# State-space taps within a chunk: 64-row matmuls on the layout of U instead of block-diagonal ones

## The chip, the cores and the metric

The kernel runs on one core of one Trainium2 chip. The metric is the device time of one execution in microseconds (us), here the median of several runs. A change of less than about 0.5% of it can't be told from no change.

## What is computed

One layer of a decoder trunk on x of 256 x 1024: a projection `x @ w_in` is cut into q, k, v, z_attn, u, z_ssm and two gates; an attention branch (8 heads of 64) and a state-space branch are gated, projected, merged and normalised. The part that the change touches is the state-space branch, 32 groups of 16 channels with 64 complex states each:

```python
bu_re = jnp.einsum('bsgc,gpc->bsgp', ug, bbar_re)        # and bu_im
_, _, h_re, h_im = lax.associative_scan(combine, (a_re_t, a_im_t, bu_re, bu_im), axis=1)
y = (jnp.einsum('bsgp,gcp->bsgc', h_re, c_re.astype(f32))
     - jnp.einsum('bsgp,gcp->bsgc', h_im, c_im.astype(f32)))
y = y.reshape(B, S, W) + d_skip.astype(f32) * u.astype(f32)
```

## The kernel before, in words

**Steps.** The large products run in 80 steps or so. Each step takes one unit of weights (256 rows by 512 columns), which SP loads into one of five `raw` buffers (`load_next`, L117). ACT rounds it into `whi` (L144), DVE subtracts for the rest `wlo` (L145), both with three buffers, and TensorE does three products for one (L149, the helper `mm`, which records nearly every matmul). Step i splits the unit of step i + 2. The list `steps` holds these steps; `at(i, ...)` hangs pieces of the other work behind step i, and `AT` says where. TensorE keeps the program's order. The order of all other engines is made by a planner that simulates the kernel with priorities, the earlier in the program the higher, and with loads, splits and the evacuation of the last product (`pend`) above all else.

**The state-space branch.** Time is cut into 64 chunks (j) of 4 positions (l). `uT` holds u with channels on partitions; `s5_bounce` writes it to `scr_u` in HBM and reads it back as `U`, in which 64 partitions hold the four positions of a group's 16 channels (two halves r of 64 partitions, 8 pairs of groups each). `s5_xm` multiplies `BT` with `U` in 64 x 64 pieces of the array, `s5_x`, `s5_scan` (L492, with the decay `m4`, to which ACT writes at L488 and POOL at L489) and `s5_h` (L505 to L511) give the state `Hr`, `Hi` ahead of each chunk. `s5_kbm` (steps 27 and 28) computes the taps within a chunk, from one position to a later one of the same chunk, into a PSUM tile `kp`. `s5_kbd` (DVE, L424 and L428) spreads them to `Kbd`: for each of the four 128-channel tiles t and each distance a block-diagonal 128 x 128 matrix, with the skip term `dk` on its diagonal. `s5_yt(t)` multiplies them with `uT` and `s5_y(t)` adds the part from `Hr`, `Hi` through `CAb` (a zero-filled spread of `CA`, L433 and L436); GELU and a split to `yh`, `yl` follow. `s5_yt` and `s5_y` of the four tiles stand by turns behind steps 35 to 42.

**Around it.** In the same stretch of the program, steps 23 to 35, the attention runs: `a_scores`, `a_exp` (L587, L592 on ACT), `a_tr` (transposes, evacuated by ACT at L602 to `pt`) and `a_out`. The tag of a tile names its memory: tiles of one tag take turns in it, so `Kbd` waits until the scores have read `kl`, and `gl` of `a_out` has the tag `kT`.

Of the kernel before, what the change touches and what calls it, by code (L numbers as in the profile page):

```python
# [10 lines left out]
F32 = mybir.dt.float32  # L11
# [3 lines left out]
AF = mybir.ActivationFunctionType  # L15
ALU = mybir.AluOpType
AX = mybir.AxisListType

P = 128
S = 256  # L20
# [3 lines left out]
L = 4  # L24
NJ = S // L
# [7 lines left out]
AT = dict(bt=24, x=27, sc=23, kb=27, cb=29, tr=31, out=32, y=35)  # L33
# [10 lines left out]


C_ID, C_MK, C_J, C_OH = 0, P, P + 8, P + 8 + NPH
C_W = C_OH + 257


def bc(ap, axis, n):  # L50

    dims = [list(d) for d in ap.ap]
    dims.insert(axis, [0, n])
    return bass.AP(tensor=ap.tensor, offset=ap.offset, ap=dims)
# [3 lines left out]
def hybrid_layer_kernel(ctx: ExitStack, tc, xT, x, pT, w_in, w_ap, w_sp, w_out, par, bp, cp,  # L58
                        dsk, w_glu, w_pg, w_pp, lng, lnb, relb, cst, out):
    nc = tc.nc  # L60
    V, A, G, PE = nc.vector, nc.scalar, nc.gpsimd, nc.tensor
    pool = ctx.enter_context(tc.tile_pool(name="sb", bufs=1))
    ps = ctx.enter_context(tc.tile_pool(name="ps", bufs=1, space=bass.MemoryType.PSUM))
    dr = ctx.enter_context(tc.tile_pool(name="dr", bufs=1, space=bass.MemoryType.DRAM))
    cnt = [0]

    def T(shape, tag, dt=F32, bufs=1, nm=None):
        cnt[0] += 1
        return pool.tile(list(shape), dt, name=f"{nm or tag}_{cnt[0]}", tag=tag, bufs=bufs)

    def PS(tag, bufs):
        cnt[0] += 1
        return ps.tile([P, 512], F32, name=f"{tag}_{cnt[0]}", tag=tag, bufs=bufs)
# [4 lines left out]
    def aux():  # L78
        return PS("aux", 4)
# [9 lines left out]

    cs = T([P, C_W], "cst")  # L90
    ident = cs[:, C_ID:C_ID + P]
    mask = cs[:, C_MK:C_MK + 8]
# [55 lines left out]
    def mm(o, a, b, start, stop):  # L148
        return PE.matmul(o, a, b, start=start, stop=stop, skip_group_check=True)  # L149
# [34 lines left out]
    for c in range(4):  # L184
        t = T([P, 2, 512], "raw", bufs=NRAW)
# [21 lines left out]
    dk = T([P, 4], "dk")  # L207
# [23 lines left out]
    st5 = {}  # L231
# [176 lines left out]
    def s5_kbm(hf):  # L408
        if hf == 0:
            st5["kp"] = aux()  # L410
        p_ = st5["kp"]
        bd = st5["bd"]
        for t in range(2 * hf, 2 * hf + 2):
            for part in range(2):
                for gpt in range(4):
                    gp = 4 * t + gpt
                    mm(p_[32 * gpt:32 * gpt + 32, 64 * t:64 * t + 64], bd[:, part, gp, :],
                       st5[f"CA{part}"][:, gp, 0:4, :].rearrange("p n c -> p (n c)"),
                       part == 0, part == 1)

    def s5_kbd():
        p_ = st5["kp"]
        kb = st5["Kbd"] = T([P, 4, 4, P], "Kbd")
        V.tensor_tensor(out=kb.rearrange("p t u (g c) -> p (t u) g c", c=16),  # L424
                        in0=bc(p_[:, 0:256].rearrange("p (tu c) -> p tu c", c=16), 2, 8),
                        in1=bc(bc(mask, 1, 16), 3, 16), op=ALU.mult)
        for t in range(4):
            V.scalar_tensor_tensor(kb[:, t, 0, :], ident, dk[:, t:t + 1], kb[:, t, 0, :],  # L428
                                   op0=ALU.mult, op1=ALU.add)

    def s5_cabd(part):
        o = st5[f"CAb{part}"] = T([P, GP, 4, 32], f"CAb{part}")
        G.memset(o, 0.0)  # L433
        for g2 in range(2):
            rw = slice(64 * g2, 64 * g2 + 64)
            A.activation(o[rw, :, :, 16 * g2:16 * g2 + 16], st5[f"CA{part}"][rw, :, 1:5, :], AF.Copy)  # L436

    uT = T([P, 4, L, NJ], "uT")
    U = T([P, 8, 2, NJ], "U")
# [73 lines left out]
    yh = []  # L513
    yl = []

    def s5_yt(t):
        p_ = st5[f"yp{t}"] = aux()
        kb = st5["Kbd"]
        for tau in range(4):
            n = (4 - tau) * NJ  # L520
            mm(p_[:, tau * NJ:4 * NJ], kb[:, t, tau, :],
               uT[:, t, 0:4 - tau, :].rearrange("p l j -> p (l j)"), tau == 0, False)

    def s5_y(t):
        p_ = st5[f"yp{t}"]
        for l in range(L):
            for part, hk in ((0, "Hr"), (1, "Hi")):
                for gpt in range(4):
                    gp = 4 * t + gpt
                    mm(p_[32 * gpt:32 * gpt + 32, l * NJ:(l + 1) * NJ],  # L530
                       st5[f"CAb{part}"][:, gp, l, :], st5[hk][:, gp, :], False, l == 3 and part == 1)
        if t == 0:
            st5["y"] = T([P, 4, S], "U")
            yh.append(T([P, 4, S], "sn", F32R))
            yl.append(T([P, 4, S], "co", F32R))
        y = st5["y"]
        A.activation(y[:, t, :].rearrange("p (j l) -> p l j", l=L),
                     p_[:, 0:256].rearrange("p (l j) -> p l j", l=L), AF.Gelu)
        A.activation(yh[0][:, t, :], y[:, t, :], AF.Copy)
        V.tensor_sub(yl[0][:, t, :], y[:, t, :], yh[0][:, t, :].bitcast(F32))  # L540
# [65 lines left out]
    def a_out(hp):  # L606
        p_ = aux()
        for i in range(2):
            h = 2 * hp + i
            t = aT[h]  # L610
            rw = slice(64 * i, 64 * i + 64)
            mm(p_[rw, 0:256], vN[:, 0, 64 * h:64 * h + 64], t[:, 0:256], True, False)
            mm(p_[rw, 128:256], vN[:, 1, 64 * h:64 * h + 64], t[:, 256:384], False, True)
        if hp == 0:
            gh.append(T([P, 4, S], "qT", F32R))
            gl.append(T([P, 4, S], "kT", F32R))
        g = T([P, S], "gf", bufs=2)
        V.scalar_tensor_tensor(g, p_[:, 0:256], 0.5, zaT[:, hp, :], op0=ALU.mult, op1=ALU.mult)
        A.activation(gh[0][:, hp, :], g, AF.Copy)
        V.tensor_sub(gl[0][:, hp, :], g, gh[0][:, hp, :].bitcast(F32))  # L620
# [208 lines left out]
    def at(i, *f):  # L829
        order.setdefault(i, []).extend(f)  # L830
# [22 lines left out]
    for hp in range(4):  # L853
        at(AT["sc"] + hp, lambda hp=hp: a_scores(hp))
        at(AT["sc"] + 1 + hp, lambda hp=hp: a_exp(hp))
    at(AT["kb"], lambda: s5_kbm(0))
    at(AT["kb"] + 1, lambda: s5_kbm(1), s5_kbd)
    at(AT["cb"], lambda: s5_cabd(0), lambda: s5_cabd(1))
    for hp in range(4):
        at(AT["tr"] + hp, lambda hp=hp: a_tr(2 * hp), lambda hp=hp: a_tr(2 * hp + 1))  # L860
        at(AT["out"] + hp, lambda hp=hp: a_out(hp))
    for t in range(4):
        at(AT["y"] + 2 * t, lambda t=t: s5_yt(t))
        at(AT["y"] + 1 + 2 * t, lambda t=t: s5_y(t))
    at(44, load_x)

    pend = None
# [36 lines left out]
    nm = [T([P, 1], f"nm{s}") for s in range(2)]  # L904
# [36 lines left out]
    u = nmain  # L941
# [26 lines left out]
def _constants():  # L968
    c = np.zeros((P, C_W), np.float32)
    c[:, C_ID:C_ID + P] = np.eye(P, dtype=np.float32)  # L970
    c[:, C_MK:C_MK + 8] = (np.arange(P)[:, None] // 16 == np.arange(8)[None]).astype(np.float32)
    c[:, C_J:C_J + NPH] = np.concatenate([np.arange(5), L * np.arange(NJ)]).astype(np.float32)
    for d in range(257):
        b = d if d < 16 else min(31, 16 + int(math.log(d / 16) / math.log(8) * 16))
        c[b, C_OH + d] = 1.0
    return c


def _layout(i):
    a = lambda t: np.ascontiguousarray(np.asarray(t))  # L980
    x = a(i["x"])[0]
    gp = lambda t: t.reshape(GP, P).T
    ldt = np.broadcast_to(a(i["ssm_log_dt"])[0][:, None], (32, 64))
    par = np.stack([gp(a(i["ssm_a_re"])[0]), gp(a(i["ssm_a_im"])[0]), gp(ldt)], axis=1)
    gb = lambda t: t.reshape(GP, P, 16).transpose(1, 0, 2)
    bp = np.stack([gb(a(i["ssm_b_re"])[0]), gb(a(i["ssm_b_im"])[0])], axis=1)
    gc = lambda t: gb(t.transpose(0, 2, 1))
    cp = np.stack([gc(a(i["ssm_c_re"])[0]), gc(a(i["ssm_c_im"])[0])], axis=1)
    return dict(
        xT=a(x.T.reshape(KD, P, S).transpose(1, 0, 2)), x=a(x),  # L990
        pT=a(a(i["p"])[0, 0].T.reshape(2, P, S).transpose(1, 0, 2)),
        w_in=a(i["w_in"])[0], w_ap=a(i["w_attn_proj"])[0], w_sp=a(i["w_ssm_proj"])[0],
        w_out=a(i["w_out"])[0], par=a(par), bp=a(bp), cp=a(cp),
        dsk=a(a(i["ssm_d"])[0].reshape(4, P).T), w_glu=a(i["w_glu"])[0],
        w_pg=a(i["w_ple_gate"])[0], w_pp=a(i["w_ple_proj"])[0],
        lng=a(i["ln_g"]), lnb=a(i["ln_b"]), relb=a(i["rel_bias"]), cst=_constants())
# [15 lines left out]
```

## Time and profile before

| | |
|---|---|
| runs | 241.4, 241.86, 242.76 us; median 241.86 us |
| profiled execution | 242.09 us, span 240.3 us, granted TensorE clock 0.995 |
| TensorE busy | 230.3 us, 96% of the span, 2042 matmuls |
| DVE busy | 188.2 us, 78% |
| ACT busy | 140.2 us, 58% |
| POOL busy | 15.9 us, 7% |
| HBM traffic | 44 MB, 183 GB/s |

Read it by stages: the shares are means over stretches in which different engines end last. A float32 matmul is recorded as two instructions, one of the rounded kind (fp32r) as one. The span leaves out 1.8 us that lie around it in the profiled execution.

### The profile page before, as it was taken

The numbers are of one execution on the slowest core, as the hardware profiler recorded it, in microseconds if no ns is written. First come the engines' busy times: TensorE is split into PE (matmuls) and PEld (weight loads), VectorE is DVE, ScalarE is ACT, GpSimd is POOL, SyncE is SP. The second block draws the span as 40 slices with busy tenths as digits, with TensorE's granted clock in tenths as the row PEclk, the third lists the DMA queues.
The fourth block names the chain that finished last, engine by engine and source line by source line (L and its number), as shares of the span: only waits on it lengthen the run. The fifth ranks groups of instructions, "written<-read, shape, count | busy, mean of one in ns | idle before, by whom it ended". The sixth has DMA issues, their size and how long they took to land.

```text
span 240.3 us, 5066 instructions
## 1 busy us (share of the span) xinstructions
PE 230.3 (96%) x2042; PEld 212.6 (88%) x2042; DVE 188.2 (78%) x333; ACT 140.2 (58%) x222; POOL 15.9 (7%) x17
## 2 busy tenths in 40 slices
PE   8899999999999999999999999999999999999970
PEld 6899999999978899998998999999888889988760
DVE  2879999999899986878999744485674479997395
ACT  4847554845588389999734955335565353775021
POOL 4000000000000005000000000072000000000031
PEclk9999999999999999999999999999999999999998
DMA  5999998977634484323743663664555655660013
GB/s 162 331 343 357 354 238 242 353 232 215 196 93 118 147 255 119 110 92 97 232 150 136 207 213 110 197 245 162 189 174 191 199 202 170 186 190 0 3 44 131
DMA packets 26374, 44.37 MB, mean 185 GB/s; under 512 B 4200, under 2 KB 7280, under 8 KB 26352
## 3 DMA queue, kind: packets, MB, share of 16 engines
q1 hardware_dynamic: 26064, 43.75, 57.5%
q8 instruction: 16, 0.26, 0.4%
q10 hardware_dynamic: 288, 0.31, 0.4%
q14 instruction: 6, 0.05, 0.1%
HBM read 42.47 MB, written 1.59 MB: 183 GB/s over the span
## 4 chain that ended last, share of the span: by engine, by line
PE 77%; ACT 10%; DMA 5%; DVE 4%; SPq 2%; issue 1%; ACTq 0%
PE acc L149 68%; PE aux L149 8%; DMA raw<-in_w_in 5%; ACT whi L144 4%; ACT sc L587 2%; ACT sc L592 2%; ACT CAb L436 1%; DVE wlo L145 1%; SPq L191 1%; SPq L189 1%; DVE xb L930 1%; DVE xb L920 1%; DVE st L910 1%; DVE xb L908 1%; PE aux L598 0%
## 5 line engine op out<-in xcount | busy, mean ns | idle before, releaser
L144 ACT ACTIVATE whi<-raw 128x1024 fp32r<-128x1024 f32 (+2 forms) x71 | 70.7, 997 | 59.9 <-PE acc L149 52.9
L145 DVE TENSOR_TENSOR wlo<-raw,whi 128x1024 fp32r<-128x1024 f32 (+2 forms) x71 | 81.9, 1154 | 30.3 <-ACT whi L144 29.9
L149 PE MATMUL acc<-xh,whi 128*128 128x256 f32 x288 | 47.7, 287 | 0.8 <-ACT whi L144 0.8
L149 PE MATMUL acc<-xl,whi 128*128 128x256 f32 x288 | 45.8, 281 | 0.0
L149 PE MATMUL acc<-xh,wlo 128*128 128x256 f32 x288 | 45.6, 280 | 0.0
L149 PEld LDWEIGHTS acc<-xh,whi 128*128 128x128 f32 x288 | 39.3, 190 | 2.3 <-ACT whi L144 1.3
L149 PEld LDWEIGHTS acc<-xl,whi 128*128 128x128 f32 x288 | 39.3, 189 | 0.0
L149 PEld LDWEIGHTS acc<-xh,wlo 128*128 128x128 f32 x288 | 38.9, 188 | 0.3 <-DVE wlo L145 0.3
L149 PE MATMUL acc<-whi,xh 128*128 128x512 f32 x48 | 19.0, 395 | 0.0
L149 PE MATMUL acc<-wlo,xh 128*128 128x512 f32 x48 | 19.0, 395 | 0.0
L149 PE MATMUL acc<-whi,xl 128*128 128x512 f32 x48 | 19.0, 395 | 0.0
L149 PEld LDWEIGHTS acc<-wlo,xh 128*128 128x128 f32 x48 | 9.0, 188 | 2.2
L149 PEld LDWEIGHTS acc<-whi,xh 128*128 128x128 f32 x48 | 9.0, 188 | 2.1
L149 PEld LDWEIGHTS acc<-whi,xl 128*128 128x128 f32 x48 | 9.0, 188 | 2.1
L149 PE MATMUL acc<-whi,BT 128*128 128x512 f32 (+1 forms) x32 | 9.1, 366 | 0.0
L818 POOL TENSOR_SCALAR xb<-xb 128x1024 f32<-128x1024 f32 x2 | 5.5, 2774 | 42.2 <-DMA xb<-in_x 42.2
L916 ACT ACTIVATE rs<-mv,eps 128x1 f32<-128x1 f32 x2 | 0.6, 294 | 12.1 <-DVE mv L915 12.1
L587 ACT ACTIVATE sc<-sc,nmx 128x128 f32<-128x128 f32 (+1 forms) x16 | 7.0, 442 | 0.0
L149 PEld LDWEIGHTS acc<-whi,BT 128*128 128x128 f32 x32 | 5.7, 188 | 1.1
L193 DVE TENSOR_TENSOR xl<-sc,xh 128x256 fp32r<-128x256 f32 x8 | 3.4, 420 | 4.1 <-ACT xh L192 4.1
L908 DVE TENSOR_TENSOR xb<-acc,xb 128x512 f32<-128x512 f32 (+1 forms) x4 | 2.5, 619 | 5.0 <-PE acc L149 5.0
L928 POOL TENSOR_TENSOR xb<-xb,lng 128x512 f32<-128x512 f32 (+1 forms) x2 | 1.7, 839 | 69.8 <-ACT xb L927 69.8
(254 smaller groups left out, 407.8 us busy)
## 6 DMA issues: line engine op xcount, KB each, us to landing
raw<-in_w_in SPq DMA_DIRECT2D x36, 512.0 KB, 4.7
raw<-in_w_pg SPq DMA_DIRECT2D x8, 512.0 KB, 4.6
raw<-in_w_out SPq DMA_DIRECT2D x8, 512.0 KB, 4.5
raw<-in_w_ap SPq DMA_DIRECT2D x4, 512.0 KB, 5.0
raw<-in_w_glu SPq DMA_DIRECT2D x4, 512.0 KB, 3.9
raw<-in_w_sp SPq DMA_DIRECT2D x4, 512.0 KB, 4.1
raw<-in_w_in SPq DMA_DIRECT2D x7, 256.0 KB, 4.3
sc<-in_xT SPq DMA_DIRECT2D x8, 128.0 KB, 4.0
```

The costliest lines, as they stand in the source:

```text
L144: A.activation(h[:, k, c], r[:, k, c], AF.Copy)
L145: V.tensor_sub(l[:, k, c], r[:, k, c], h[:, k, c].bitcast(F32))
L149: return PE.matmul(o, a, b, start=start, stop=stop, skip_group_check=True)
L189: nc.sync.dma_start(xs[:, kk], xT[:, kk])
L191: nc.sync.dma_start(t[:, k, cc], units[c][:, k, cc])
L193: V.tensor_sub(xl[:, kk], xs[:, kk], xh[:, kk].bitcast(F32))
L436: A.activation(o[rw, :, :, 16 * g2:16 * g2 + 16], st5[f"CA{part}"][rw, :, 1:5, :], AF.Copy)
L587: A.activation(sc[:, h, qs[q]], sc[:, h, qs[q]], AF.Exp, bias=nmx[:, h, q:q + 1], accum_out=sm_[:, h, q:q + 1])
L592: A.activation(sc[:, h, qs[q]], sc[:, h, qs[q]], AF.Copy, scale=sm_[:, h, q:q + 1])
L818: G.tensor_scalar(late["xb"][:, s, :], late["xb"][:, s, :], ALPHA, None, op0=ALU.mult)
L908: V.tensor_tensor(out=xb[:, s, sl], in0=(yo2 if c0 else yo[s][n])[:, 0:c1 - c0], in1=xb[:, s, sl], op=ALU.add)
L910: V.bn_stats(out=stat[s][:, c // 256, :], in_=xb[:, s, c:c + 256])
```

## The change

The taps no longer make a block-diagonal matrix. `s5_kt` lays them out by ACT as `kt` (one row of 256 numbers for each position l, zero where the distance is negative; POOL zeroes it first), DVE adds the skip term, SP writes it to HBM (`scr_k`), and eight DMAs issued from POOL read it back as `tt`, whose 64-partition halves match those of `U`, beside a zeroed half. `s5_yt(t0)` handles tiles t0 and t0 + 2 at once: for each l, half of a pair of groups (g2), pair and r a matmul with 64 rows, 32 columns and 64 moving columns, alternately on the upper and the lower half of the array and into two PSUM tiles. The zeros in `tt` fill the 16 of the 32 columns that belong to the other group. `y` takes the memory of `uT` instead of `U`, and the tiles come in the order 0, 2, 1, 3.

```diff
--- before.py
+++ after.py
@@ -44,7 +44,8 @@
 
 
 C_ID, C_MK, C_J, C_OH = 0, P, P + 8, P + 8 + NPH
-C_W = C_OH + 257
+C_M16 = C_OH + 257
+C_W = C_M16 + 16
 
 
 def bc(ap, axis, n):
@@ -418,15 +419,30 @@
                        st5[f"CA{part}"][:, gp, 0:4, :].rearrange("p n c -> p (n c)"),
                        part == 0, part == 1)
 
-    def s5_kbd():
-        p_ = st5["kp"]
-        kb = st5["Kbd"] = T([P, 4, 4, P], "Kbd")
-        V.tensor_tensor(out=kb.rearrange("p t u (g c) -> p (t u) g c", c=16),
-                        in0=bc(p_[:, 0:256].rearrange("p (tu c) -> p tu c", c=16), 2, 8),
-                        in1=bc(bc(mask, 1, 16), 3, 16), op=ALU.mult)
+    kscr = dr.tile([512, 4, 64], F32, name="scr_k")
+
+    def s5_kt():
+
+        p_ = st5["kp"][:, 0:256].rearrange("p (t u c) -> p t u c", t=4, u=4)
+        kt = T([P, 4, 4, 16, 4], "kT", nm="kt")
+        G.memset(kt, 0.0)
+        for l in range(L):
+            A.activation(kt[:, :, l, :, l:4].rearrange("p t c u -> p t u c"), p_[:, :, 0:4 - l, :],
+                         AF.Copy)
+        m16 = bc(cs[:, C_M16:C_M16 + 16], 1, 4)
         for t in range(4):
-            V.scalar_tensor_tensor(kb[:, t, 0, :], ident, dk[:, t:t + 1], kb[:, t, 0, :],
-                                   op0=ALU.mult, op1=ALU.add)
+            d = kt[:, t, 0, :, 0]
+            d = bass.AP(tensor=d.tensor, offset=d.offset, ap=[list(d.ap[0]), [65, 4], list(d.ap[1])])
+            V.scalar_tensor_tensor(d, m16, dk[:, t:t + 1], d, op0=ALU.mult, op1=ALU.add)
+        nc.sync.dma_start(kscr.rearrange("(t q) l d -> q t (l d)", q=P),
+                          kt.rearrange("q t l c u -> q t (l c u)"))
+        tt = st5["tt"] = T([P, 16, 2, 64], "Kbd", nm="tt")
+        G.memset(tt[:, :, 1, :], 0.0)
+        v = kscr.rearrange("(r m c) l d -> r l c m d", r=2, c=16)
+        for r in range(2):
+            for l in range(L):
+                b0 = 64 * r + 16 * (L - 1 - l)
+                nc.gpsimd.dma_start(tt[b0:b0 + 16, :, 0, :], v[r, l])
 
     def s5_cabd(part):
         o = st5[f"CAb{part}"] = T([P, GP, 4, 32], f"CAb{part}")
@@ -513,13 +529,21 @@
     yh = []
     yl = []
 
-    def s5_yt(t):
-        p_ = st5[f"yp{t}"] = aux()
-        kb = st5["Kbd"]
-        for tau in range(4):
-            n = (4 - tau) * NJ
-            mm(p_[:, tau * NJ:4 * NJ], kb[:, t, tau, :],
-               uT[:, t, 0:4 - tau, :].rearrange("p l j -> p (l j)"), tau == 0, False)
+    def s5_yt(t0):
+
+        for t in (t0, t0 + 2):
+            st5[f"yp{t}"] = aux()
+        tt = st5["tt"].rearrange("p m z d -> p (m z d)")
+        for l in range(L):
+            for g2 in range(2):
+                for gpt in range(4):
+                    for r in range(2):
+                        t = t0 + 2 * r
+                        gpp = 4 * (t % 2) + gpt
+                        rw = slice(64 * r, 64 * r + 64)
+                        o = 128 * (2 * gpp + g2) - 64 * g2 + l
+                        mm(st5[f"yp{t}"][32 * gpt:32 * gpt + 32, l * NJ:(l + 1) * NJ],
+                           tt[rw, o:o + 125:4], U[rw, gpp, g2, :], l == 0 and g2 == 0, False)
 
     def s5_y(t):
         p_ = st5[f"yp{t}"]
@@ -529,8 +553,8 @@
                     gp = 4 * t + gpt
                     mm(p_[32 * gpt:32 * gpt + 32, l * NJ:(l + 1) * NJ],
                        st5[f"CAb{part}"][:, gp, l, :], st5[hk][:, gp, :], False, l == 3 and part == 1)
-        if t == 0:
-            st5["y"] = T([P, 4, S], "U")
+        if "y" not in st5:
+            st5["y"] = T([P, 4, S], "uT", nm="y")
             yh.append(T([P, 4, S], "sn", F32R))
             yl.append(T([P, 4, S], "co", F32R))
         y = st5["y"]
@@ -854,14 +878,15 @@
         at(AT["sc"] + hp, lambda hp=hp: a_scores(hp))
         at(AT["sc"] + 1 + hp, lambda hp=hp: a_exp(hp))
     at(AT["kb"], lambda: s5_kbm(0))
-    at(AT["kb"] + 1, lambda: s5_kbm(1), s5_kbd)
+    at(AT["kb"] + 1, lambda: s5_kbm(1), s5_kt)
     at(AT["cb"], lambda: s5_cabd(0), lambda: s5_cabd(1))
     for hp in range(4):
         at(AT["tr"] + hp, lambda hp=hp: a_tr(2 * hp), lambda hp=hp: a_tr(2 * hp + 1))
         at(AT["out"] + hp, lambda hp=hp: a_out(hp))
-    for t in range(4):
-        at(AT["y"] + 2 * t, lambda t=t: s5_yt(t))
-        at(AT["y"] + 1 + 2 * t, lambda t=t: s5_y(t))
+    for t in range(2):
+        at(AT["y"] + 4 * t, lambda t=t: s5_yt(t))
+        at(AT["y"] + 1 + 4 * t, lambda t=t: s5_y(t))
+        at(AT["y"] + 3 + 4 * t, lambda t=t: s5_y(t + 2))
     at(44, load_x)
 
     pend = None
@@ -970,6 +995,7 @@
     c[:, C_ID:C_ID + P] = np.eye(P, dtype=np.float32)
     c[:, C_MK:C_MK + 8] = (np.arange(P)[:, None] // 16 == np.arange(8)[None]).astype(np.float32)
     c[:, C_J:C_J + NPH] = np.concatenate([np.arange(5), L * np.arange(NJ)]).astype(np.float32)
+    c[:, C_M16:C_W] = (np.arange(P)[:, None] % 16 == np.arange(16)[None]).astype(np.float32)
     for d in range(257):
         b = d if d < 16 else min(31, 16 + int(math.log(d / 16) / math.log(8) * 16))
         c[b, C_OH + d] = 1.0
```

## Rows read from the trace of the kernel before

**Rows 1.** The page, part 1: busy us, share of span, instructions, by engine.

```profile
PE 230.3 (96%) x2042; PEld 212.6 (88%) x2042; DVE 188.2 (78%) x333; ACT 140.2 (58%) x222; POOL 15.9 (7%) x17
```

**Rows 2.** The chain that ended last: start, length in us, what.

```profile
91.78 1.39 ACT sc L592 x4
...
102.72 0.95 ACT CAb L436
...
108.00 1.07 ACT whi L144
...
112.35 0.38 ACT pt L602
...
112.77 1.24 PE aux L149 x7
...
156.78 61.37 PE acc L149 x372
```

**Rows 3.** Windows: busy us (instructions) by engine, PEclk, DMA share, GB/s.

```profile
108.00:112.00 4.00, 4.00 (x36) 4.00 (x36) 2.91 (x4) 4.00 (x7) 0.00 (x0) 1.00 0.13 18
112.00:116.00 4.00, 3.77 (x31) 3.21 (x30) 4.00 (x6) 3.32 (x7) 0.12 (x1) 1.00 0.84 253
```

**Rows 4.** Timeline of PE, stage of y: start us, us, matmul groups.

```profile
130.93 0.63 PE L149 MATMUL acc<-xh,wlo 128*128 128x256 f32 x4
131.49 1.10 PE L149 MATMUL aux<-BT,CAb 128*32 128x64 f32 x64
132.52 0.74 PE L149 MATMUL acc<-xh,whi 128*128 128x256 f32 x4
...
134.99 0.63 PE L149 MATMUL acc<-xh,wlo 128*128 128x256 f32 x4
135.46 1.31 PE L149 MATMUL aux<-uT,Kbd 128*128 128x256 f32 x8
136.57 0.70 PE L149 MATMUL acc<-xh,whi 128*128 128x256 f32 x4
```

**Rows 5.** Timeline of PE, the 64 x 64 matmuls on U.

```profile
101.67 0.69 PE L149 MATMUL aux<-U,BT 64*64 64x64 f32 x32
102.30 0.74 PE L149 MATMUL acc<-xh,whi 128*128 128x256 f32 x4
```

**Rows 6.** Timeline of PE, the tap matrices themselves.

```profile
98.07 0.65 PE L149 MATMUL aux<-C,Bbd 128*32 128x64 f32 x32
98.65 0.74 PE L149 MATMUL acc<-xh,whi 128*128 128x256 f32 x4
```

**Rows 7.** Lines of ACT by form, 60 to 160 us: busy us, mean ns.

```profile
L592 ACT ACTIVATE sc<-sc,sms 128x256 f32<-128x256 f32 x8 | 4.0, 494 | 0.0
...
L592 ACT ACTIVATE sc<-sc,sms 128x128 f32<-128x128 f32 x8 | 3.1, 387 | 0.0
...
L537 ACT ACTIVATE U<-aux 128x256 f32<-128x256 f32 x4 | 2.6, 640 | 1.4 <-PE aux L149 1.4
```

**Rows 8.** Timeline of DVE: the spreading to Kbd, the scan, the state.

```profile
100.78 2.28 DVE L424 TENSOR_TENSOR Kbd<-aux,cst 128x2048 f32<-128x2048 f32 x1
...
104.17 1.13 DVE L428 SCALAR_TENSOR_TENSOR Kbd<-cst,dk,Kbd 128x128 f32<-128x128 f32 x4
...
117.54 2.28 DVE L492 TENSOR_TENSOR_SCAN A<-B,A 128x1024 f32<-128x1024 f32 x1
...
129.73 0.68 DVE L511 TENSOR_TENSOR BT<-BT,Ct 128x512 f32<-128x512 f32 x1
```

**Rows 9.** Tile U: its DMA issues (ns min/median/max, first/last start us), landing.

```profile
L449 SPq DMA_DIRECT2D U<-scr_u x8: 302/442/590, 27.8 to 34.1; - x8
...
DMA to landing us min/median/max: 4.9/6.6/7.8
```

**Rows 10.** DMA issues: count, KB each, median us to landing.

```profile
scr_u<-uT SPq DMA_DIRECT2D x1, 512.0 KB, 5.7
```

**Rows 11.** Timeline of POOL.

```profile
115.62 0.12 POOL L489 MEMSET B<- 128x16 f32 x1 [21.60 <-DVE A L482]
```

## The prediction

> **What bounds the kernel now.** I read the busy shares first: TensorE is busy 96% of the span and no other engine over 78% [rows 1], at a granted clock of 0.995, its upper level. So what counts is first how long TensorE works on the taps, and then whether a moved instruction makes it wait. For the second the chain that ended last tells where TensorE is not alone: it runs along ACT from 91.78 (and a little before) to 112.73, through the exponentials' scaling (L592), the `CAb` copies (L436), a weight split (L144) and `pt` (L602), and only then goes over to TensorE at 112.77 [rows 2]. The windows say how tight this is: from 108 to 112 both ACT and TensorE are busy for all 4.00 us; from 112 to 116 TensorE is busy 3.77, that is, it waited 0.23 us, for `pt` [rows 3]. Before this point every microsecond given to ACT is one that TensorE waits; after it ACT has room (3.32 of 4 us). From 156.78 on the chain is TensorE for 61 us [rows 2], and nothing of the change lies there.
>
> **What the taps cost now.** One `s5_yt` is 8 instructions, from 135.46 to the next step's first matmul at 136.57: 1.11 us. They stream 2 x (256 + 192 + 128 + 64) = 1280 columns, 0.87 ns each, one after the other. The group behind it takes 0.70 instead of 0.63 [rows 4]. So about 1.18 us a tile, 4.7 us for four.
>
> **What they cost after.** 256 recorded instructions with 64 moving columns each, which by 0.87 ns would take 56 ns alone, 14 us in all. They needn't run alone. `s5_y` issues 64 of that moving length, 32 columns wide, to four column strips by turns, and takes 1.03 us, from 131.49 to 132.52 [rows 4]; the tap matrices take 0.58 us for 32 of the same shape, 98.07 to 98.65 [rows 6]. So 8 turns of four take 0.45 us, 56 ns a turn, as long as one alone: four run at once. Do the upper and the lower 64 rows run at once too? The 64 x 64 matmuls on `U` say so: two row halves by two column halves by turns, 32 in 0.63 us [rows 5]; one row half at a time would be 16 turns, 0.9 us. So I take eight at once, which no row shows as such: the 128 instructions of one `s5_yt` are 16 turns, as in `s5_y`, 1.03 us. A change of the array's division costs at both ends: the group behind `s5_y` takes 0.74 for 0.63, and `s5_y` begins 131.49 where the rhythm of a group (134.99 to 135.46, 0.47) from 130.93 on would have it at 131.40 [rows 4]; 8 turns of the 64-row form took 0.63 against 0.58 [rows 5, 6]. That is 1.03 + 0.11 + 0.09 + 0.05 = 1.28 us, twice 2.5 to 2.6. **TensorE gains 4.7 - 2.5 = 2.2 us.** If only four run at once, each call has 16 more turns of 56 ns: 4.3 us, a gain of 0.4. Strided weights (every fourth number of `tt`) appear in no row; I price them at nothing, since the turns are set by the moving columns, and the four-at-once case is their upper bound.
>
> A rule of the Trainium skill speaks against so many small matmuls: the page "TensorE: Matmul & The Clock Gate", section "Wait — 56ns, not 53.3ns?", has for one matmul a floor of about 25 ns from start to start. By it 256 would take 6.4 us, and the change would lose 1.7 us instead. The trace does not agree: 64 in 1.03 us are 16 ns [rows 4].
>
> **What ACT gets.** Four copies out of PSUM, of 256, 192, 128 and 64 columns (the rows l of `kt`), behind `s5_kbm(1)`. L592 takes 0.494 for 256 columns and 0.387 for 128 [rows 7], so by a straight line 0.44 for 192 and 0.33 for 64, 1.65 us together; back to back four of L592 (two of each size, 1.76 busy) take 1.39 in the chain [rows 2], 0.09 less apiece. So 1.65 - 0.37 = 1.3 us. The writes go to every fourth number; L537, which writes so too and also computes GELU, takes 0.640 for 256 [rows 7], 1.3 times as much: upper bound 1.7. Where do they stand? `kp` is ready at about 98.7 [rows 6], and in the program they come before `CAb`, `a_tr` and thus before `pt`, so the planner will put them before `pt` wherever exactly. There ACT has no gap. **TensorE waits 1.3 us more** (bounds 0 and 1.7; 0 if four copies of like size, such as `CAb`, are put behind `pt` in return).
>
> **What DVE gets.** It loses 2.28 us of L424 and 1.13 of L428 [rows 8] and gets four of 64 columns for the four of 128 of L428, so it gains between 2.28 and 3.41 us. In that stretch the chain is ACT's [rows 2], so it is worth nothing on the path.
>
> **What SP and POOL get.** SP: one issue to `scr_k`, 512 KB, which waits for `kt`. Behind it stand weight loads. With five buffers and a split two steps ahead of use the load of a unit may start three steps before its split, and a step is some 4 us here (130.93 to 134.99 with what lies between [rows 4]): the wait is covered up to about 12 us less a landing, and would cost TensorE whatever lies above. POOL: two memsets in a stretch where it is idle (21.60 us ahead of L489 [rows 11]), then eight loads which wait for `scr_k`, and behind them, as I expect of the planner, the memset of `m4` at L489 (115.62 now [rows 11]), on which the scan at 117.54 depends [rows 8]. Timing: `kt` is written by ACT by about 109.3 and by DVE by 110.5. The bounce of u to `scr_u` took 5.7 us to land [rows 10]: 116.2. An issue of the eight loads to `U` took SP 0.442 us [rows 9]; no row shows one on POOL, and I take the same: 3.5 us, POOL is free at 119.7. The loads land 6.6 us after issue [rows 9]: 126.3. TensorE wants them at 127.3 + 1.3 = 128.6. The scan would have been at 118.8 and is 0.9 us late; the first half of the state is ready at 130.41 (L511 [rows 8]) and wanted at 131.49, so 1.1 us late costs nothing. Both just fit. I take **0**, with -0 and +4 as bounds (below).
>
> **The sum.** -2.2 + 1.3 + 0 = -0.9 us. The profiled execution, 242.09 with 1.8 us outside its span, becomes 241.2; it lies 0.23 above the median of 241.86, which becomes **241.0**. The rest of the program, stream of weights and tail, is as before: `y` in the memory of `uT` is free long before, and the last tile comes behind the same step 42.
>
> **Rivals.**
> *ACT's copies cost nothing.* For it: the planner orders by simulated time, and the real ACT is behind it; four `CAb` copies, 0.95 us and more each [rows 2], are wanted only at 131. If some move behind `pt`, or the taps' copies do, the whole 2.2 us stay: 239.7. Against: the program's order, by which `kt` comes before `CAb` and `pt`.
> *Four at once.* If a row half waits for the other (both write the same partitions, of two PSUM banks), the gain is 0.4: 241.86 - 0.4 + 1.3 = 242.8. Against: rows 5.
> *POOL is the bound (slower).* If an issue costs POOL 1 us in place of 0.44, it is free at 124.2; the scan, and with it all that is queued behind it on DVE, starts 5.3 us late, `s5_y(0)` waits 5.3 - 1.1 = 4.2 us, and the loads, landing by 130.8, cost `s5_yt(0)` 2.2 of these already. That gives 245. It decides from 0.5 us per issue, or `scr_k` landing 0.3 us later: close. Against: the planner could put the memset first, or the wait could be half of it, 243.
>
> The Trainium skill has a rule for this rival, on the page "SBUF — State Buffer", section "SBUF: two separate sides": the descriptors of a DMA issued from GpSimd are written by GpSimd itself, and a DVE instruction in a two-port mode keeps it from its port meanwhile. By it the loads could be held off where DVE is busy all the time, as from 112 to 116 [rows 3], and the time would be that of this rival; no run here shows a load from POOL yet.
>
> **Chances.** Main case 0.40 (240.4 with half of ACT's cost hidden, 241.6 with its upper bound and a short wait), ACT free 0.22, four at once 0.10, POOL late 0.28. The line for faster is 240.65, for slower 243.07, which is the 0.5% that can be told from no change. Faster: 0.22 + 0.10 of the main case = 0.32. Slower: 0.24 of POOL late + 0.04 = 0.28. Within: 0.40. The range leaves out the far end of POOL late and a little below the best case: 239.4 to 244.5.
>
> **What would show it.** TensorE: 128 matmuls of 64 x 32 per call in about 1.03 us (1.9 if four at once). ACT: four copies before `pt`, and TensorE's wait ahead of `a_out(0)` growing from 0.23 to 1.5 us. POOL: eight issues between 116 and 120, L489 behind them, no wait of TensorE ahead of steps 35 and 36. I am wrong if the planner reorders this stage at large, or if the row halves exclude each other.

## The result and the profile after

The changed kernel takes 245.25 us (median of 4 runs, 244.16 to 245.81) against 241.76 us; the ratio is 1.0128, 95% interval 1.0093 to 1.0162 (the quotient of two medians, here 1.0144, differs a little from the ratios given here and below and lies within their intervals). It is slower, and above my range of 239.4 to 244.5. The profiled execution took 245.81 us (before: 242.09), with a span of 243.6 us and a granted clock of 0.991.

The first part of the page, to be held against [rows 1]: 224 matmuls more, yet TensorE is busy 0.9 us less and its share falls from 96% to 94%. It works less and waits more.

```profile
PE 229.4 (94%) x2266; PEld 210.2 (86%) x2266; DVE 186.5 (77%) x332; ACT 141.7 (58%) x226; POOL 23.3 (10%) x27
```

What it waits for, from 92 to 165 us, by releaser: us in total, times, longest. Before, this list had one entry, 0.2 us for `pt`, the 0.23 us of [rows 3].

```profile
PE acc L150 <- ACT whi L145: 1.2, 1, 1.2
PE aux L150 <- DVE BT L523: 0.6, 1, 0.6
PE acc L150 <- DVE wlo L146: 0.5, 1, 0.5
PE aux L150 <- DVE BT L527: 0.5, 1, 0.5
PE acc L150 <- issue: 0.5, 1, 0.5
```

So there are three places. I lay the two traces side by side from the first `U,BT` block (93.21 before, 94.03 after) to the stretch of 372 matmuls that nothing of the change touches (156.78 and 160.12): 63.6 us before, 66.1 after, 2.5 more, and 61.37 us for the stretch in both [rows 2]. Cut by blocks on TensorE, from a block's first start to the next one's:

| us | before | after | difference |
|---|---|---|---|
| transposes, step 32, `a_out(0)` | 5.06 | 6.97 | +1.91 |
| taps (four calls; two calls) | 4.58 | 3.15 | -1.43 |
| step behind `s5_yt(0)` and `s5_y(0)` | 4.04 | 5.36 | +1.32 |
| step behind `s5_yt(2)`; behind `s5_yt(1)` | 3.02 | 3.81 | +0.79 |
| all other blocks | | | -0.08 |

The first and the last of these blocks begin and end with the starts of the following lines of TensorE, before and then after (the last line is cut short by its view's window, which ends at 153):

```profile
108.88 0.27 PE L598 MATMUL aux<-cst,sc 128*128 128x128 f32 x1
113.94 0.33 PE L598 MATMUL aux<-cst,sc 128*128 128x128 f32 x1
...
144.56 0.72 PE L149 MATMUL acc<-qT,whi 128*128 128x256 f32 x4
147.58 1.10 PE L149 MATMUL aux<-BT,CAb 128*32 128x64 f32 x64
```
```profile
109.60 0.27 PE L622 MATMUL aux<-cst,sc 128*128 128x128 f32 x1
116.57 0.33 PE L622 MATMUL aux<-cst,sc 128*128 128x128 f32 x1
...
148.31 0.74 PE L150 MATMUL acc<-qT,whi 128*128 128x256 f32 x4
152.12 1.09 PE L150 MATMUL aux<-BT,CAb 128*32 128x64 f32 x63
```

The other 1.2 us of the two profiled executions are 0.8 us in the first 94 us and 0.4 us outside the span. The first `U,BT` block stands at 92.6 to 93.2 us in the four profiles of the kernel before and of runs made from it, and at 92.8 to 94.0 in the ten of the changed kernel and its variants, 94.0 being the highest. TensorE's waits for `whi` in the first 90 us are 1.8 us here and 0.8 before, but 0.8 to 1.4 us over the first four profiles and 0.5 to 2.0 over the ten: at least part of the 0.8 us is the scatter of single executions. The 0.4 us outside the span are not: all four executions of the changed kernel have 2.1 to 2.2 us there, and 31 of the kernel before, those timed with run 1, have 1.7 to 1.8. What makes them, no run shows.

**First place.** ACT (start us, us, what), before and then after:

```profile
108.00 1.06 ACT L144 ACTIVATE whi<-raw 128x1024 fp32r<-128x1024 f32 x1
108.97 1.48 ACT L592 ACTIVATE sc<-sc,sms 128x128 f32<-128x128 f32 x4
```
```profile
103.53 4.25 ACT L452 ACTIVATE CAb<-C 64x1024 f32<-64x1024 f32 x4
107.79 1.09 ACT L750 ACTIVATE Bbd<-acc 128x512 f32<-128x512 f32 x2
108.76 1.36 ACT L430 ACTIVATE kt<-aux 128x256 f32<-128x256 f32 x4
110.14 0.80 ACT L616 ACTIVATE sc<-sc,sms 128x128 f32<-128x128 f32 x2
110.85 1.04 ACT L145 ACTIVATE whi<-raw 128x1024 fp32r<-128x1024 f32 x1
```

Before, the split `whi` of this step began at 108.00, right behind `Bbd`. Now the four copies into `kt` and two of the exponentials' scalings (L616, the line 592 of before) stand ahead of it. TensorE is out of work at 110.71:

```profile
111.94 0.74 PE L150 MATMUL acc<-xh,whi 128*128 128x256 f32 x4 [1.23 <-ACT whi L145]
...
113.68 0.74 PE L150 MATMUL acc<-xh,wlo 128*128 128x256 f32 x4 [0.53 <-DVE wlo L146]
```

**Second place.** POOL's loads, `m4`, and then DVE's queue up to the two operands that `s5_y(0)` waits for:

```profile
114.60 4.64 POOL L445 DMA_DIRECT2D tt<-scr_k  x8 [18.87 <-DMA scr_k<-kt]
119.23 0.15 POOL L505 MEMSET B<- 128x16 f32 x1
```
```profile
119.31 0.42 DVE L642 SCALAR_TENSOR_TENSOR gf<-aux,zaT 128x256 f32<-128x256 f32 x1
120.93 1.23 DVE L146 TENSOR_TENSOR wlo<-raw,whi 128x1024 fp32r<-128x1024 f32 x1 [1.20 <-ACT whi L145]
122.07 0.42 DVE L642 SCALAR_TENSOR_TENSOR gf<-aux,zaT 128x256 f32<-128x256 f32 x1
122.41 0.42 DVE L644 TENSOR_TENSOR kT<-gf,qT 128x256 fp32r<-128x256 f32 x1
122.97 0.42 DVE L644 TENSOR_TENSOR kT<-gf,qT 128x256 fp32r<-128x256 f32 x1 [0.15 <-ACT qT L643]
123.32 4.46 DVE L508 TENSOR_TENSOR_SCAN A<-B,A 128x1024 f32<-128x1024 f32 x2
...
135.16 0.69 DVE L527 TENSOR_TENSOR BT<-BT,Ct 128x512 f32<-128x512 f32 x1
```

The memset is done at 119.38, but the scan begins at 123.32: DVE's order is the planner's, fixed beforehand, and in it the scan, which had begun at 117.54 [rows 8], now stands behind a split, two gates and two products. L527 (the line 511 of before) comes 5.4 us later than in [rows 8].

**Third place, and the taps.** TensorE:

```profile
129.89 1.64 PE L150 MATMUL aux<-U,tt 64*32 64x64 f32 x128
131.46 0.72 PE L150 MATMUL acc<-xh,whi 128*128 128x256 f32 x4
...
135.06 0.32 PE L150 MATMUL aux<-BT,CAb 128*32 128x64 f32 x8 [0.61 <-DVE BT L523]
135.90 0.99 PE L150 MATMUL aux<-BT,CAb 128*32 128x64 f32 x56 [0.53 <-DVE BT L527]
...
149.84 0.28 PE L150 MATMUL acc<-qT,whi 128*128 128x256 f32 x1
150.62 0.62 PE L150 MATMUL acc<-qT,whi 128*128 128x256 f32 x3 [0.51 <-issue]
```

A call takes 1.57 us (129.89 to 131.46). At 150 us TensorE stands still with nothing that it waits for. From 148 to 150 us the DMA queues show what else went on, a block of instruction code being loaded:

```profile
q8 instruction: 1, 0.02, 3.0%
```

Whether that holds TensorE up isn't shown: in the eighth run such a block came at 145.97, in its second call of the taps, and TensorE did not stand still there.

### The profile page after: what moved, and what is told of

Read it like the earlier page. It is cut to its first block, busy times and chain, and to the rows that moved or that the text cites. A ratio compares the mean times of both kernels' runs of the same rounds, so it can differ in the third digit from the quotient of the medians.

```text
span 243.6 us, 5557 instructions
## 1 busy us (share of the span) xinstructions
PE 229.4 (94%) x2266; PEld 210.2 (86%) x2266; DVE 186.5 (77%) x332; ACT 141.7 (58%) x226; POOL 23.3 (10%) x27
## 4 chain that ended last, share of the span: by engine, by line
PE 72%; ACT 9%; DVE 8%; DMA 7%; SPq 2%; issue 1%; ACTq 0%; DVEq 0%
PE acc L150 66%; PE aux L150 5%; DMA raw<-in_w_in 5%; ACT whi L145 2%; ACT sc L611 2%; DVE wlo L146 2%; DMA Ct<-in_pT 2%; ACT CAb L452 2%; ACT sc L616 2%; SPq L192 1%; SPq L190 1%; DVE xb L955 1%; DVE xb L945 1%; DVE st L935 1%; DVE xb L933 1%
## 5 line engine op out<-in xcount | busy, mean ns | idle before, releaser
L842 POOL TENSOR_SCALAR xb<-xb 128x1024 f32<-128x1024 f32 x2 | 6.5, 3276 | 37.7 <-DMA xb<-in_x 37.7
```

The source lines that it names most:

```text
L842: G.tensor_scalar(late["xb"][:, s, :], late["xb"][:, s, :], ALPHA, None, op0=ALU.mult)
```

## The experiments

Theory A: the four copies on ACT make TensorE wait for the splits, and by making `kt` late they make POOL's loads, `m4` and the scan late too; the taps themselves gain. Theory B, the first rival: the loads on POOL alone are to blame. Theory C: the matmuls are not worth what they seem, or bring costs of their own. Times beside before's on the same chip; "ACT stretch" is the first row of the table above (5.06 before, 6.97 after).

**1. The taps alone.** `s5_kt` cut down to a zeroed `tt`: no copies on ACT, no skip term, no transfers, so the taps' part of the result is left out.

```diff
-        kt = T([P, 4, 4, 16, 4], "kT", nm="kt")
...
-        G.memset(tt[:, :, 1, :], 0.0)
...
+        G.memset(tt, 0.0)
```

> The new taps without their preparation: the four copies to kt, the skip term, the write to HBM and the eight loads are left out, tt is zeroed once, so y lacks the taps within a chunk. It shows what TensorE gains by itself. Theory A (the loss is in the preparation: ACT, the order on DVE, POOL): TensorE waits no more than in the kernel before ahead of a_out(0) and ahead of s5_y(0), each call of s5_yt takes 1.57 us as in the changed kernel, so two calls take 3.1 us for 4.6 before: 240.3 us, 1.5 below the kernel before. Rival B (the small matmuls themselves cost what is lost, in what follows them): 243 to 245 us.

Measured: 241.64 us against 241.90, ratio 0.9978 (0.9958 to 0.9997). The two calls take 3.15 us and nothing waits at `s5_y(0)`, but the ACT stretch is 5.61, not 5.06, and the step behind `s5_yt(1)` has 0.4 us more. So the taps do gain 1.4 us, and something other than the copies takes 0.55 of it back. ACT shows where: all four scalings now stand ahead of `whi`, which before went first.

```profile
108.00 1.50 ACT L596 ACTIVATE sc<-sc,sms 128x128 f32<-128x128 f32 x4
109.40 2.94 ACT L145 ACTIVATE whi<-raw 128x1024 fp32r<-128x1024 f32 x3
```

**2 to 4. `m4` on DVE, the copies on DVE, both.** In the changed kernel:

```diff
-        G.memset(m4[:, :, 0:1], 0.0)
+        V.memset(m4[:, :, 0:1], 0.0)
```
```diff
-            A.activation(kt[:, :, l, :, l:4].rearrange("p t c u -> p t u c"), p_[:, :, 0:4 - l, :],
-                         AF.Copy)
+            V.tensor_copy(kt[:, :, l, :, l:4].rearrange("p t c u -> p t u c"), p_[:, :, 0:4 - l, :])
```

> The zero column of m4 is written by DVE instead of POOL, all else as in the changed kernel; so the scan no longer depends on POOL behind its eight issues, and the planner may put it earlier on DVE. Theory A (s5_y(0) waited because the scan was planned late for POOL's sake): the scan starts 2 to 3 us earlier against its step, TensorE's two waits in s5_y(0), 0.61 and 0.53 us, go, and the time is 1.1 to 1.3 us below the changed kernel, 244.0. Rival (the state is late because DVE is full, whatever POOL does): the waits stay, 245.2.

> The four copies from PSUM to kt are done by DVE instead of ACT, all else as in the changed kernel. Theory A (TensorE's waits ahead of step 32, 1.23 and 0.53 us, come from the four copies in ACT's full queue, 1.3 us, and from DVE's wait for them ahead of the weights' rest): these waits shrink to 0.5 us in all, 243.9 to 244.3. Rival (the stage is late for another reason, the order as a whole): no change, 245.2.

> Both edits: copies to kt and the zero column of m4 on DVE. If the two waits are separate and each theory holds: the sum of both gains, 2.2 to 2.6 us, 242.6 to 243.0, still not below the kernel before. If one wait takes the place of the other: 243.9 or more.

Measured: 243.88, 242.19 and 242.22 us (ratios 1.0058, 1.0001 and 1.0007, each within 0.0036). With `m4` on DVE the waits at `s5_y(0)` are gone and those in the ACT stretch stay. With the copies on DVE both are gone (0.5 us of waiting for `whi` is left, 0.9 in the fourth run), though `m4` is still POOL's and still behind the loads:

```profile
108.36 4.64 POOL L444 DMA_DIRECT2D tt<-scr_k  x8 [13.84 <-DMA scr_k<-kt]
115.13 0.13 POOL L504 MEMSET B<- 128x16 f32 x1 [2.13 <-DVE A L497]
```

The loads start 6.2 us sooner, and the memset waits for DVE, not for them. This is more than I expected of the third run (243.9 to 244.3): both losses hang on the same four copies, and the fourth run adds nothing. Theory B falls as it stands: the loads are the same, and begun sooner they no longer hurt. That they hurt when they are late, by keeping `m4` behind them, is what the second run shows.

The second run shows one thing more, and its time is near the 244.0 that I expected in part by luck. After the same two waits (1.23 and 0.53 us) its groups of four come 0.86 us apart, against 0.47, and the granted clock falls (columns as in [rows 3]; the first row is of the changed kernel, the second of this run):

```profile
112.00:116.00 4.00, 3.47 (x26) 3.10 (x28) 4.00 (x6) 3.82 (x7) 1.40 (x3) 1.00 0.64 197
```
```profile
112.00:116.00 4.00, 3.47 (x19) 3.22 (x20) 4.00 (x6) 2.98 (x5) 2.52 (x5) 0.63 0.65 207
```

Step 32 took 5.06 us there against 3.82. A wait of this size may thus cost 1.2 us on top, by TensorE being put to its lower level (1.2 GHz) for part of it, or may not. The profiled execution of the second run thus gained 1.3 us at `s5_y(0)` and 0.8 where the changed kernel stood still at 150 us, and lost 1.3 in the ACT stretch.

**5 to 7. `CAb` behind `pt`.** A small DVE instruction that reads the first `pt` writes the 1.0 by which the `CAb` copies multiply; in the changed kernel, in the same with the copies into `kt` on DVE, and in the kernel before. The copies' place in the program goes from step 29 to step 32 with it.

```diff
+            V.tensor_scalar(st5["one"], aT[0][:, 0:1], 0.0, 1.0, op0=ALU.mult, op1=ALU.add)
...
-            A.activation(o[rw, :, :, 16 * g2:16 * g2 + 16], st5[f"CA{part}"][rw, :, 1:5, :], AF.Copy)
+            A.activation(o[rw, :, :, 16 * g2:16 * g2 + 16], st5[f"CA{part}"][rw, :, 1:5, :], AF.Copy,
+                         scale=st5["one"][rw])
```

> The changed kernel with one thing moved: the four CAb copies are made to wait for the first pt (a small DVE instruction that reads pt writes the scale they multiply by), so that ACT does them behind pt and the four kt copies no longer come on top of CAb ahead of it. Theory A (ACT's extra copies stand ahead of the splits and of pt, TensorE waits there, and the same delay makes kt, the loads from POOL and thus the scan late): in the changed kernel CAb takes ACT 4.25 us ahead of kt, so all behind it is some 4 us earlier: the waits of 1.23 us on whi and 0.53 us on wlo ahead of step 32 go (that stretch 6.97 falls to 5 to 5.5 us), the waits of 1.1 us in and ahead of s5_y(0) go or fall below 0.3, and the time is 242.0 to 242.8 us. Rival C (the two losses have other causes, such as the loads from POOL holding DVE or SP's queue): waits stay, 245 us.

> As the run before, and the four copies into kt by DVE in place of ACT, so that ACT has less ahead of pt than in the kernel before. Theory A: the stretch with the transposes, step 32 and a_out(0) is at most that of the kernel before, 5.06 us, perhaps 4.6; no wait at s5_y(0); taps 1.43 us less than before; instruction loading costs 0.4 to 0.5 us. So 240.6 to 241.1 us, about 1 us under the kernel before. Rival: what is gained on ACT comes back as a wait for DVE (wlo), as it did with m4 on DVE: 242.2, as with the DVE copies alone.

> The kernel before with the CAb copies behind pt and nothing else: it tells how much of the run before is not the change's. Theory A: TensorE waited 0.2 to 0.6 us for ACT in that stretch of the kernel before, which goes; 241.2 to 241.6 us. Rival: no difference, 241.8, since DVE's wlo ends last there anyway.

Measured: 245.94, 244.94 (the median of three; a fourth took 247.17) and 245.78 us against 241.74, all slower (ratios 1.0177, 1.0128 and 1.0175, each within 0.0073); I was wrong by 3 to 5 us in each. The ACT stretch did fall, to 4.28, 4.28 and 4.39 us, and `s5_y(0)` no longer waits. But ACT does the four copies in one go, and the next `pt` waits behind them, here in the kernel before with that edit (ACT, then TensorE's waits):

```profile
113.82 4.62 ACT L439 ACTIVATE CAb<-C,one 64x1024 f32<-64x1024 f32 x4
118.46 0.87 ACT L606 ACTIVATE pt<-aux 128x384 f32<-128x384 f32 x2
```
```profile
PE aux L149 <- ACT pt L606: 2.5, 1, 2.5
```

After it the granted clock was 0.57 from 120 to 124 us. The wait is there with and without the change (3.6, 2.8 and 2.5 us in the three runs): it came from my edit. In the sixth run's profiled execution (243.12 us, the lowest of four) the clock was 0.992; the three others had 0.980 to 0.986 and took 244.9 to 247.2.

**8 and 12. Why a call takes 1.57 us.** The loops of `s5_yt` turned round, so that one row half goes first, and the weights read side by side (so that other taps are used in place of the right ones):

```diff
-                for gpt in range(4):
-                    for r in range(2):
+                for r in range(2):
+                    for gpt in range(4):
```
```diff
-                           tt[rw, o:o + 125:4], U[rw, gpp, g2, :], l == 0 and g2 == 0, False)
+                           tt[rw, o:o + 32], U[rw, gpp, g2, :], l == 0 and g2 == 0, False)
```

> The changed kernel with the two row halves of the taps one after the other instead of by turns (the four column strips still by turns), for each l and half of a group pair. Theory P (up to 64 instructions are taken at the eight-at-once rate, 62 ns per eight, from what is queued; the rest come at some 12 ns each because issuing limits them): runs of four on one row half change little while issuing limits, a call of 128 takes 1.6 to 1.8 us against 1.57, the first 32 slower than 0.30 us (0.35 to 0.55). Rival Q (the array limits: the row halves only partly overlap): 128 matmuls at 56 ns per four are 1.8 to 1.9 us.

> The changed kernel with the weights of the taps' matmuls read from 32 neighbouring numbers in place of every fourth (so other taps are used). Theory P (beyond the first 32 the matmuls come at 12 ns each because the engine's instructions don't come faster, which the run with the row halves one after the other supports: 1.56 us in another order): 1.57 us as before. Rival S (loading weights with a stride is what takes the time): 1.0 to 1.2 us a call. The stall of 0.5 to 0.8 us behind s5_yt(1) is there or not, whichever the loading of instruction code makes it in this execution.

Measured: 244.03 and 246.65 us, a single execution of each; a call takes 1.56 us with the halves apart, against 1.57 by turns, and 1.41 without the stride. In the changed kernel and in the eighth run the first 32 matmuls of a call start within 0.30 us (I had expected 0.35 to 0.55 with the halves apart), and the other 96 take 1.27 us, 13 ns each on average. TensorE of the eighth run:

```profile
128.99 1.63 PE L150 MATMUL aux<-U,tt 64*32 64x64 f32 x128
130.55 0.74 PE L150 MATMUL acc<-xh,whi 128*128 128x256 f32 x4
```

So neither the order nor, but for a tenth, the stride sets the rate. That what remains is the pace of the engine's 256 instructions, 128 matmuls and as many weight loads, is the explanation left over; no run here measures it by itself. The stall behind `s5_yt(1)` came and went: none in the eighth run (3.03 us for the step), 0.75 us in the twelfth, in programs that differ by an order or a stride. The third run has two, 0.31 us there and 0.43 in the middle of its first call.

**10. `s5_yt` alone, with the work for `Kbd` kept.** The kernel before, whose L424 and L428 are left as they are, with the new order of the tiles and the new place of `y`; the new matmuls read what they make, which are not the taps that belong there.

```diff
-            mm(p_[:, tau * NJ:4 * NJ], kb[:, t, tau, :],
+        tt = st5["Kbd"].rearrange("p t u c -> p (t u c)")
...
+                        mm(st5[f"yp{t}"][32 * gpt:32 * gpt + 32, l * NJ:(l + 1) * NJ],
+                           tt[rw, o:o + 125:4], U[rw, gpp, g2, :], l == 0 and g2 == 0, False)
```

> The kernel before with s5_yt of the changed kernel and nothing else of it: the matrices of L424 and L428 are still made on DVE, and the new matmuls read them, in place of the taps that belong there; no kt, no copies on ACT, no transfer. It differs from the run with the taps alone by the 3.4 us of DVE's work, which that run had lost. Theory A (with this work gone, DVE's reciprocal comes earlier and the planner puts the exponentials' scaling, 1.5 us, ahead of a split on ACT, which cost 0.55 us): the stretch with the transposes and step 32 is as in the kernel before, 5.0 to 5.1 us (5.61 with the taps alone), the taps 1.43 us less, 0 to 0.8 us of stall behind s5_yt(1): 240.6 to 241.3 us. Rival (the 0.55 us come from something else that the matmuls bring): 5.6 us there, 241.6.

Measured: 241.67 us against 242.07, ratio 0.9971 (0.9946 to 0.9995); the profiled execution took 240.18, the lowest of ten (up to 242.51), and what the others lost stands in no trace. The median is thus the rival's 241.6. The trace is as theory A has it: the ACT stretch is 4.87 us, no longer than before, with `whi` ahead of the scalings again, and this order is the program's and the same in every execution. DVE, first in this run and then in the changed kernel:

```profile
99.99 2.28 DVE L424 TENSOR_TENSOR Kbd<-aux,cst 128x2048 f32<-128x2048 f32 x1
102.19 0.17 DVE L597 RECIPROCAL sms<-sms 128x4 f32<-128x4 f32 x1
```
```profile
101.09 0.67 DVE L493 TENSOR_TENSOR A<-aux,sn 128x504 f32<-128x504 f32 x1
101.68 0.17 DVE L613 RECIPROCAL sms<-sms 128x4 f32<-128x4 f32 x1
```

The scalings need that reciprocal. Without `Kbd` ahead of it it is ready sooner, the planner finds the scalings ready sooner, and puts them ahead of a split that TensorE wants first. That is the 0.55 us: work taken away from an engine off the path. That `Kbd` decides the order is shown by the two runs (1 without it, 10 with it); that it does so through the reciprocal is read from the program, as no run moved the reciprocal alone.

**9 and 11. `CAb` one by one.** The changed kernel with the copies into `kt` on DVE and each `CAb` copy behind another `pt` (steps 31, 32, 33, 33), held back by an instruction on ACT itself; and the kernel before with the same `CAb` edit. (The `CAb` edit in the changed kernel with the copies into `kt` still on ACT was not run.)

```diff
+        A.activation(one, aT[hh][:, 0:1], AF.Copy, scale=0.0, bias=1.0)
...
+    for n, (stp, hh) in enumerate(((31, 1), (32, 3), (33, 4), (33, 5))):
+        at(stp, lambda n=n, hh=hh: s5_cabd(n // 2, n % 2, hh))
```

> The changed kernel with the four copies into kt on DVE, and the four CAb copies on ACT one by one behind the pt of steps 31, 32 and 33 (a small ACT instruction that reads pt writes the scale they multiply by, so DVE isn't held). The runs that moved all four CAb behind one pt took the waits ahead of step 32 away (4.28 us for that stretch against 6.97), and put them back as one of 2.8 us for a later pt, since ACT did the four together. Theory A: one by one they fit into ACT's gaps of 0.5 to 1.8 us in each step: the stretch stays at 4.3 to 4.5 us, later steps are as in the kernel before, taps are 1.43 us less, nothing waits at s5_y(0): 240.0 to 240.8 us. Rival: any CAb copy behind pt costs its 1.06 us in the next step: 241.5 to 242.5.

> The kernel before with the CAb copies one by one behind pt, as in the ninth run: what that edit gives without the change. Theory A: TensorE's waits for ACT ahead of step 32 go there too, 5.06 to 4.4 us; 241.0 to 241.4 us, so that the changed taps are worth 0.6 to 1 us with the same edit on both sides. Rival: DVE, which still has Kbd to make, ends last there: 241.8.

Measured: 240.22 and 242.71 us against 242.07: ratios 0.9921 (0.9891 to 0.9951) and 1.0024 (1.0006 to 1.0042). The ninth run beats both kernels, by 0.8% the one before. From 92 to 165 us its list of waits is empty; the ACT stretch is 4.28 us, the scan begins at 115.70, and the taps keep their gain (POOL, DVE and TensorE of the ninth run):

```profile
113.78 0.13 POOL L509 MEMSET B<- 128x16 f32 x1
```
```profile
115.70 4.46 DVE L512 TENSOR_TENSOR_SCAN A<-B,A 128x1024 f32<-128x1024 f32 x2
```
```profile
126.62 1.64 PE L150 MATMUL aux<-U,tt 64*32 64x64 f32 x128
128.19 0.74 PE L150 MATMUL acc<-xh,whi 128*128 128x256 f32 x4
```

The same edit does not help the kernel before: its ACT stretch falls to 4.39 us too, but the stretch up to the 372 matmuls is 0.4 us longer, and behind `s5_yt(0)` TensorE now waits for an evacuation on ACT. I had expected 241.0 to 241.4. In ACT's order that evacuation stands behind a gate's `qT`, for which ACT waited 1.49 us until DVE had `gf` ready, and behind a split; why DVE is later there was not followed further. TensorE of the eleventh run:

```profile
128.08 0.99 PE L149 MATMUL acc<-xh,whi 128*128 128x256 f32 x4 [0.54 <-ACT ts L731]
```

## Why the prediction was wrong, by its own steps

- **What bounds the kernel**: right. TensorE's waits in the ACT stretch decided, and ACT's queue ahead of `pt` was the place. But what TensorE waited for there were the splits of step 32 (`whi` 1.23 us, `wlo` 0.53), not `pt`, as I had it.
- **Taps on TensorE, 2.2 us**: the direction was right, the size was not. I took 1.03 us for the 128 matmuls of a call from the rate of 64 in `s5_y`, and 1.28 with what a change of the array's division costs at the ends. The first 32 do come eight at once, near the price assumed (0.30 us; 0.26 by the prediction), but 128 in a row take 1.57. The gain is 1.43 us: the term was 0.8 us too large. The rule of the Trainium skill that I weighed there ("TensorE: Matmul & The Clock Gate", "Wait — 56ns, not 53.3ns?", about 25 ns from start to start) would have made a call 3.2 us. The trace does not agree: a call took 1.57 us, 12.3 ns a matmul on average.
- **ACT, 1.3 us**: right. The copies took 1.36 us, and the changed kernel's stretch is 1.36 us longer than the one without them (6.97 against 5.61).
- **DVE, nothing**: wrong by 0.55 us. I looked at the path and saw that DVE isn't on it; but the reciprocal stood behind the work that goes, and ACT's order changes when that work is gone (runs 1 and 10).
- **POOL and SP, nothing**: here the prediction broke. POOL was free at 119.2 us, where I had 119.7, and that was luck: `scr_k` was issued at 111.4 for 110.5 and an issue on POOL took 0.58 us for 0.44, but the bounce took 2.9 for 5.7. The loads were in time, as forecast (the last landed at 126.2, `s5_yt(0)` began at 129.9), and so was SP. The step that failed is "the scan 0.9 us late": I let the scan start as soon as `m4` is there, while DVE's order is fixed beforehand, with five other instructions ahead of it. I had it start at 119.7; it began at 123.32, 5.8 us later than before, and cost 1.32 us, the largest of the four terms that I had wrong. The rival "POOL is the bound" named this chain of events and 245 us, and lay nearest; but its price (4.2 us at `s5_y(0)`) was three times too high, and the loads on POOL are not the root: run 3 has them all, at the same 0.58 us each, and loses nothing at `s5_y(0)`.
- **TensorE standing still with nothing to wait for**: not in the sum at all. The step behind `s5_yt(1)` took 0.79 us more; in the runs with the new taps it was between 0 and 0.9 us, with 0.7 more in the first call of run 3. TensorE has 448 instructions more, matmuls and weight loads, and instruction code was loaded nearby, but the cause stays open, for such loads come without a stall too.

Put in, the terms give -1.43 + 1.36 + 0.55 + 1.32 + 0.79 - 0.08 = 2.5 us, the measured lengthening of the stretch, where I had -0.9. Of the 3.5 us between the medians about one stays open: the start and what lies outside the span (0.8 and 0.4 us in the profiled pair). The clock fell in runs 2 and 12 after the waits that the changed kernel has too, but not in its own profiled execution, and its four executions, with a granted clock of 0.991 to 0.994, show no sign of it.

The other rule that I weighed (the Trainium skill, "SBUF — State Buffer", "SBUF: two separate sides"), by which DVE would hold off loads issued from POOL while it is in a two-port mode, is neither borne out nor refuted, as no run here shows that mode. That DVE is busy made no difference: eight issues took 4.64 us with DVE busy all the time (the ninth run, 109.12 to 113.76) as with DVE busy 2.3 of 4 us (the third, from 108.36).

## What to carry to other kernels

A piece of work that moves from one engine to another moves the order of both: ask not only whether the copies fit but what was standing behind the work that goes, and what a planner will now find ready first. When a wait is charged to a resource (POOL's loads here), follow its input one step back before mending it; taking four copies off the crowded engine cured two losses that looked independent. And work that is put behind a marker should be spread, for four copies in one go behind `pt` cost more than they had ahead of it (a wait of 2.5 us in the kernel before, for 0.7 us of ACT stretch).

## What the runs showed of the hardware

In the changed kernel 64-row, 32-column matmuls of 64 moving columns start 7 ns apart within a group of eight, and the groups come 62 ns apart (the second 109 ns behind the first), for the first 32 of a call; from there on they came 13 ns apart on average, in either order of the row halves. Eight DMA issues on POOL, of 64 KB each, took 0.56 to 0.75 us each; they landed 3.8 to 7.9 us after issue in the changed kernel and 3.0 to 4.7 in the third run. After nearly the same two waits (1.23 and 0.53 us) the granted clock from 112 to 116 us was 1.00 in two profiles (the changed kernel and the eighth run) and 0.63 and 0.69 in two others (the second and the twelfth).
